# Up projections of a Mamba-2 and attention decoder: hi and lo of the input in one 512-column matmul, the two weights in banks of two pools

## The chip, the cores and the metric

The kernel runs on 1 core of one Trainium2 chip. The metric is the device time of one execution in microseconds; the median of 3 runs stands for the kernel.

## What is computed

A decoder of two layers on 256 tokens of width 1024, in float32. Each layer is a SwiGLU FFN (half step), a token mixer and another FFN; the mixer is a Mamba-2 scan in the first layer and sliding-window attention in the second. The change concerns the four FFNs alone:

```python
D_MODEL, SEQ, D_FF = 1024, 256, 2816

def swiglu_half_step(h, g, w1, w3, w2):
    u = rmsnorm(h, g)
    return h + 0.5 * ((silu(u @ w1) * (u @ w3)) @ w2)

h = swiglu_half_step(h, ...)      # layer 0, FFN 0
h = h + mamba2_mixer(...)
h = swiglu_half_step(h, ...)      # layer 0, FFN 1
k, v = shared_kv(h, ...)
h = swiglu_half_step(h, ...)      # layer 1, FFN 0
h = h + sliding_window_attention(...)
h = swiglu_half_step(h, ...)      # layer 1, FFN 1
```

## The kernel before, in words

Activations are kept transposed, features on the 128 partitions and the 256 tokens along the columns. To keep float32 accuracy every operand is split into two float32r parts, hi and lo, and a product is three matmuls: hi weight by hi input, hi weight by lo input, lo weight by hi input (`wmm3`, line 140). The input of the later up projections is split into `uTh` and `uTl` (lines 89 and 90) by `Norm.normalize` (line 291); the first two chunks use an input that is not yet normalized (`cur.vh`, `cur.vl`) and scale the result.

Weights come from HBM as 1 MB units (`Unit`, line 146) into one of 3 raw buffers, issued by SP; ScalarE casts the hi part (line 168) and VectorE subtracts to get the lo part (line 169), in pieces of 512 columns, into 8 hi and 8 lo buffers of 1024 columns.

An FFN (`run_ffn`, line 303) goes over 11 chunks of 256 hidden columns, c = 0 to 10, and two halves f of 128 columns each. For one half, `up` (line 355) makes w1 and w3 (w = 0 and 1) over eight k of 128 features. Both results share one bank of 512 columns, tile `pm`, w1 in the left half and w3 in the right. The bank comes from pool `ps_mm`, which has 2. `gate` (line 324) does silu of the left half on ScalarE (`sl`, line 330), the product with the right half on VectorE (`g`, line 332), and splits it into hi and lo, the two halves of tile `ghl` (ScalarE line 335, VectorE line 336). `flush` (line 378) then does the down projection of the half chunk before, 24 matmuls into four banks `acc`; in the last FFN it is 12 matmuls of 512 columns, with the gated product as the stationary operand and the weights streaming (`down_t`, line 372). At the end of an FFN the last two half chunks are projected down bank by bank.

A scheduler sets the order on each engine; some places are tied by hand. PSUM has eight banks: 2 of `ps_mm`, 4 of `ps_acc`, 2 of `ps_tr`. In the FFNs `ps_tr` serves small tiles only (the statistics of the norm, transposes). The core of it before the change:

```python
        def up(c, f):
            pm = ps_mm.tile([P, 512], F32, tag="mm", name=nm("pm"))
            ...
            for w in range(2):
                for k in range(KT):
                    up_one(c, f, pm, k, w, k == 0, k == KT - 1)
            return pm
```

Of the kernel before, what the change touches and what calls it, by code (L numbers as in the profile page):

```python
# [11 lines left out]
F32 = mybir.dt.float32  # L12
F32R = mybir.dt.float32r
AF = mybir.ActivationFunctionType
# [4 lines left out]
P = 128  # L19
D = 1024  # L20
KT = D // P
S = 256
# [18 lines left out]
def yoco_kernel(ctx: ExitStack, tc: tile.TileContext, a: dict, out: bass.AP):  # L41
    nc = tc.nc
    ctx.enter_context(nc.allow_low_precision("float32 operands split into float32r parts"))

    const = ctx.enter_context(tc.tile_pool(name="const", bufs=1))
# [3 lines left out]
    sb = ctx.enter_context(tc.tile_pool(name="sb", bufs=2))  # L49
    ps_mm = ctx.enter_context(tc.tile_pool(name="ps_mm", bufs=2, space=PSUM))  # L50
    ps_acc = ctx.enter_context(tc.tile_pool(name="ps_acc", bufs=4, space=PSUM))
    ps_tr = ctx.enter_context(tc.tile_pool(name="ps_tr", bufs=2, space=PSUM))
# [33 lines left out]
                            base=1 - P, channel_multiplier=1)  # L86

    hT = const.tile([P, KT, S], F32, name="hT")
    uTh = const.tile([P, KT, S], F32R, name="uTh")
    uTl = const.tile([P, KT, S], F32R, name="uTl")  # L90

    uid = [0]

    def nm(s):
        uid[0] += 1
        return f"{s}_{uid[0]}"
# [5 lines left out]
    def in_turn(op, *args, **kw):  # L102
        if strict[0]:
            with tc.issue_after(pe[-1]):
                r = op(*args, **kw)  # L105
        else:
            r = op(*args, **kw)  # L107
        pe.append(r.ins)

    def mm(o, l, r, first, last):  # L110
        in_turn(nc.tensor.matmul, o, l, r, start=first, stop=last)
# [18 lines left out]
    def tick():  # L130
        while soon and len(pe) >= soon[0][0]:
            soon.pop(0)[1]()
# [7 lines left out]
    def wmm3(o, wh, wl, uh, ul, first, last):  # L140
        mm(o, wh, uh, first, False)
        mm(o, wh, ul, False, False)
        mm(o, wl, uh, False, last)
        tick()
# [35 lines left out]
    def up_unit(w1, w3, c, half, cut=1, hold=False, between=None):  # L180
        cs = slice(c * 256, c * 256 + 256)
        n = 4 // cut
        parts = []
        for k in range(0, 4, n):
            r0 = half * 512 + k * P
            for i, w in enumerate((w1, w3)):
                parts.append((i * 256, 256, 512,
                              w[r0:r0 + n * P, cs].rearrange("(k p) c -> p k c", p=P), k))
            if between is not None and k == 0:
                parts.append(between)  # L190
        return Unit(parts, hold=hold)
# [44 lines left out]
    def two(ap):  # L236
        return ap.unsqueeze(1).to_broadcast([P, 2, S])

    def half(ap):
        return ap.rearrange("p (i s) -> p i s", i=2)  # L240
# [62 lines left out]
    def run_ffn(layer, j, cur, nxt, hook=None, ups=None, at=(60, 84), pre=None):  # L303
# [10 lines left out]
        def units(c):  # L314
            if c not in ups:
                ups[c] = [up_unit(w1, w3, c, 0), up_unit(w1, w3, c, 1)]
            return ups[c]
# [6 lines left out]
        def gate(c, pm):  # L324
            if c < 2:
                t = sb.tile([P, 512], F32, tag="cv", name=nm("tp"), bufs=2)
                nc.vector.tensor_mul(half(t), half(pm), two(cur.rb))
                pm = t
            sl = sb.tile([P, 256], F32, tag="g", name=nm("sl"), bufs=3)
            nc.scalar.activation(sl, pm[:, 0:256], AF.Silu)  # L330
            g = sb.tile([P, 256], F32, tag="g", name=nm("g"), bufs=3)
            nc.vector.tensor_mul(g, pm[:, 256:512], sl)  # L332
            ghl = sb.tile([P, 512], F32R, tag="ghl", name=nm("ghl"), bufs=4)
            gh, gl = ghl[:, 0:256], ghl[:, 256:512]
            nc.scalar.copy(gh, g)  # L335
            nc.vector.tensor_sub(gl, g, gh.bitcast(F32))
            return gh, gl

        def up_one(c, f, pm, k, w, first, stop):
            xh, xl = (cur.vh, cur.vl) if c < 2 else (uTh, uTl)  # L340
            wh, wl = units(c)[k // 4].get((k % 4) * 512 + w * 256 + f * P, P)
            wmm3(pm[:, w * 256:(w + 1) * 256], wh, wl, xh[:, k, :], xl[:, k, :], first, stop)

        def up_first():
            pms = [ps_acc.tile([P, 512], F32, tag="acc", name=nm("pm")),
                   (ps_acc if pre else ps_mm).tile([P, 512], F32, tag="acc" if pre else "mm", name=nm("pm"))]
            for k in range(KT):
                if pre and k in pre:
                    pre[k]()
                for f in range(2):  # L350
                    for w in range(2):
                        up_one(0, f, pms[f], k, w, k == 0 and w == 0, k == KT - 1 and w == 1)
            return pms

        def up(c, f):
            pm = ps_mm.tile([P, 512], F32, tag="mm", name=nm("pm"))
            if c == 1 and f == 0 and pre:
                for k in range(KT):
                    for w in range(2):
                        up_one(c, f, pm, k, w, k == 0 and w == 0, k == KT - 1 and w == 1)  # L360
# [5 lines that stand above are left out]
# [34 lines left out]
        def start_gates():  # L400
            for f in range(2):
                pend.append((0, f, gate(0, g0[f])))
            cur.normalize()

        slow = at[1] > 96
        for c in range(NCHUNK):
            for f in range(2):
                if c == 0 and f == 0:
                    later(*stats)
                    later(*scale)  # L410
                    with tc.issue_after(pe[-1]) if pe else nullcontext():
                        g0 = up_first()
                    if not slow:
                        start_gates()
                if c == 0:
                    continue
                pm = up(c, f)
                if slow and c == 1 and f == 0:
                    start_gates()
                g = gate(c, pm)  # L420
                if c < C:
                    if not (slow and c == 1 and f == 0):
                        flush(pend.pop(0))
                    if c == 1 and f == 1:
                        while pend:
                            flush(pend.pop(0))
                    pend.append((c, f, g))
                elif f == 0:
                    gc0 = g
                if c == 5 and len(gcols) == 1:  # L430
                    gain_cols(grow[1])
                if c == 5 and f == 0 and last:
                    residual()
                if c >= 3 and hook is not None:
                    next(hook, None)
# [10 lines left out]
        for t in range(NT):  # L446
            for n in range(2):
# [3 lines left out]
                o = sb.tile([P, 512], F32, tag="cv", name=nm("o"), bufs=2)  # L451
# [684 lines left out]
    def keep_x():  # L1136
# [17 lines left out]
        for b in (3, 0, 1, 2):  # L1154
# [4 lines left out]
    turn_x(0)  # L1159
    turn_x(1)  # L1160
    run_ffn(0, 0, norms[0], norms[1], ups=ups, at=(128, 142),
            pre={1: lambda: turn_x(2), 3: lambda: turn_x(3), 7: keep_x})
    xpool.close()
    with tc.tile_pool(name="mp", bufs=1) as mp:
        mamba(mp, norms[1], norms[2])
    with tc.tile_pool(name="ap", bufs=1) as ap:
        run_ffn(0, 1, norms[2], norms[3])
        kT, vtok, bias = {}, {}, {}
        run_ffn(1, 0, norms[3], norms[4], hook=shared_kv(ap, norms[3], kT, vtok, bias))
        attention(ap, norms[4], kT, vtok, bias, norms[5])  # L1170
# [40 lines left out]
```

## Time and profile before

| what | us |
| --- | --- |
| median of 3 runs | 1064.51 |
| the 3 runs | 1062.97, 1064.51, 1064.96 |
| profiled execution | 1061.67 |
| its span, first to last instruction | 1060.0 |

A name such as `pm<-uTh,wh` is the tile written and the tiles read, buffer numbers left out. PE is TensorE, PEld its weight loads, DVE VectorE, ACT ScalarE, POOL GpSimd. Matmuls overlap, so the length of one is not the time until the next starts: for the pace, divide a piece of the chain by its count, or subtract starts in the timeline. In a timeline row that merges several instructions the length is from the first start to the last end. `L107` is the line of a helper that issues nearly all matmuls, so matmuls are told apart by their tiles.

### The profile page before, as it was taken

How to read it: one execution, taken by the hardware profiler on the slowest of the kernel's cores; microseconds unless marked ns; L12 is line 12 of the kernel's file. 1: busy time of each engine (PE TensorE's matmuls, PEld its weight loads, DVE VectorE, ACT ScalarE, POOL GpSimd, SP SyncE). 2: the span in 40 equal slices, each digit the busy share in tenths (PEclk: the TensorE clock that was granted, in tenths of full speed). 3: DMA queues.
4: the chain of work that ended last, by engine and by line, in shares of the span. 5: the costliest groups of instructions: out<-in, count | busy, mean ns of one | idle time of the engine just before them, and what ended most of it. 6: DMA issues, size and time to landing. Idle time of an engine off the chain costs nothing.

```text
span 1060.0 us, 20512 instructions
## 1 busy us (share of the span) xinstructions
PE 1044.2 (99%) x8282; PEld 1006.2 (95%) x8282; DVE 701.4 (66%) x1420; ACT 582.7 (55%) x1204; POOL 53.0 (5%) x79
## 2 busy tenths in 40 slices
PE   9999999999999999999999999999999999999998
PEld 8999999989899999999999999999996699999997
DVE  6864545797899899645455974654577678454543
ACT  7553544677867656535445754454467565443541
POOL 1100000003210010000000000100002000000000
PEclk9999999999999999999999999999999999999999
DMA  8665646545456374646465556584641346463631
GB/s 290 207 211 177 207 161 219 169 146 197 147 169 222 120 194 168 199 163 221 161 213 164 195 162 198 165 297 162 213 159 41 120 136 216 149 216 124 227 127 40
DMA packets 138927, 187.34 MB, mean 177 GB/s; under 512 B 4940, under 2 KB 120816, under 8 KB 138832
## 3 DMA queue, kind: packets, MB, share of 16 engines
q1 hardware_dynamic: 136496, 179.32, 51.5%
q0 software_dynamic: 2288, 6.69, 2.2%
q8 instruction: 65, 1.06, 0.4%
q14 instruction: 30, 0.25, 0.1%
q10 hardware_dynamic: 48, 0.02, 0.0%
HBM read 184.90 MB, written 1.11 MB: 175 GB/s over the span
## 4 chain that ended last, share of the span: by engine, by line
PE 93%; DVE 4%; ACT 1%; DMA 1%; issue 1%; POOL 0%; SPq 0%; ACTq 0%; DVEq 0%; POOLq 0%
PE pm L107 47%; PE acc L107 23%; PE pp L107 8%; PE pa L107 5%; PE pq L105 2%; PE pa L105 1%; DVE wl L169 1%; PE pz L107 1%; PE py L107 1%; PE ps L105 1%; PE po L105 1%; DVE sp L961 1%; DMA xin<-in_x_dram 1%; PE pkv L107 1%; DVE zs L746 1%
## 5 line engine op out<-in xcount | busy, mean ns | idle before, releaser
L169 DVE TENSOR_TENSOR wl<-raw,wh 128x512 fp32r<-128x512 f32 x676 | 431.6, 685 | 140.9 <-ACT wh L168 140.1
L168 ACT CAST wh<-raw 128x512 fp32r<-128x512 f32 x676 | 379.1, 618 | 191.2 <-PE pm L107 89.4
L107 PE MATMUL pm<-uTh,wh 128*128 128x256 f32 x1152 | 323.2, 281 | 0.0
L107 PE MATMUL pm<-uTl,wh 128*128 128x256 f32 x1152 | 323.1, 280 | 0.0
L107 PE MATMUL pm<-uTh,wl 128*128 128x256 f32 x1152 | 323.1, 280 | 0.0
L107 PEld LDWEIGHTS pm<-uTh,wh 128*128 128x128 f32 x1152 | 217.2, 189 | 0.9 <-issue 0.2
L107 PEld LDWEIGHTS pm<-uTl,wh 128*128 128x128 f32 x1152 | 216.8, 188 | 0.6
L107 PEld LDWEIGHTS pm<-uTh,wl 128*128 128x128 f32 x1152 | 217.1, 188 | 0.0
L107 PE MATMUL acc<-ghl,wh 128*128 128x256 f32 x1056 | 190.9, 282 | 0.2 <-ACT ghl L335 0.2
L107 PEld LDWEIGHTS acc<-ghl,wh 128*128 128x128 f32 x1056 | 162.2, 188 | 0.4 <-ACT ghl L335 0.4
L107 PE MATMUL acc<-ghl,wl 128*128 128x256 f32 x528 | 148.6, 282 | 0.0
L332 DVE TENSOR_TENSOR g<-pm,sl 128x256 f32<-128x256 f32 x72 | 30.3, 421 | 134.7 <-ACT sl L330 134.7
L330 ACT ACTIVATE sl<-pm 128x256 f32<-128x256 f32 x72 | 27.4, 380 | 165.4 <-PE pm L107 165.4
L107 PEld LDWEIGHTS acc<-ghl,wl 128*128 128x128 f32 x528 | 99.4, 188 | 0.0
L107 PE MATMUL pp<-uTh,wh 128*128 128x256 f32 x288 | 81.8, 285 | 1.9 <-ACT uTh L300 1.4
L107 PE MATMUL pp<-uTl,wh 128*128 128x256 f32 x288 | 81.4, 284 | 0.4 <-DVE uTl L301 0.2
L107 PE MATMUL pp<-uTh,wl 128*128 128x256 f32 x288 | 80.8, 282 | 0.0
L107 PE MATMUL pm<-vh,wh 128*128 128x256 f32 x256 | 73.2, 286 | 0.0
L107 PE MATMUL pm<-vl,wh 128*128 128x256 f32 x256 | 72.4, 283 | 0.0
L107 PE MATMUL pm<-vh,wl 128*128 128x256 f32 x256 | 72.3, 283 | 0.0
L107 PE MATMUL acc<-wh,ghl 128*128 128x512 f32 x176 | 58.1, 394 | 0.0
L107 PEld LDWEIGHTS pp<-uTh,wh 128*128 128x128 f32 x288 | 54.4, 190 | 2.6 <-ACT uTh L300 1.5
(242 smaller groups left out, 1432.1 us busy)
## 6 DMA issues: line engine op xcount, KB each, us to landing
raw<-in_ffn_w_dram SPq DMA_DIRECT2D x168, 512.0 KB, 4.8
raw<-in_ffn_w_dram SPq DMA_DIRECT2D x44, 1024.0 KB, 5.1
raw<-in_ssm_w_in_dram SPq DMA_DIRECT2D x16, 1024.0 KB, 5.5
raw<-in_ssm_w_out_dram SPq DMA_DIRECT2D x8, 1024.0 KB, 5.2
raw<-in_ffn_w_dram SPq DMA_DIRECT2D x16, 256.0 KB, 6.0
raw<-in_ssm_w_in_dram SPq DMA_DIRECT2D x8, 512.0 KB, 5.4
pr<-pdram POOLq DMA_DIRECT2D x8, 512.0 KB, 4.6
raw<-in_w_q_dram SPq DMA_DIRECT2D x4, 1024.0 KB, 4.9
```

The lines of the kernel that those rows point to most:

```text
L105: r = op(*args, **kw)
L107: r = op(*args, **kw)
L168: return (nc.scalar.copy(wh, rs).ins, nc.vector.tensor_sub(wl, rs, wh.bitcast(F32)).ins)
L169: nc.vector.tensor_sub(wl, rs, wh.bitcast(F32)).ins)
L330: nc.scalar.activation(sl, pm[:, 0:256], AF.Silu)
L332: nc.vector.tensor_mul(g, pm[:, 256:512], sl)
L746: nc.vector.tensor_mul(zs[:, j, :], y1, zs[:, j, :])
L961: chain[1] = op(*args, **kw).ins
```

## The change

The hi and lo inputs become the two halves of one tile `uT`, side by side for each k. For chunks 2 to 10 the hi weight is multiplied with both at once, one matmul of 512 columns into a whole bank, so that the bank's left half gets hi by hi and its right half hi by lo; the lo weight by the hi input is added onto the left half by a second matmul of 256 columns. w1 and w3 then need a bank each, one of `ps_mm` and one of `ps_tr`. In the gate ScalarE copies the right half of each bank to SBUF and VectorE adds it to the left half (tile `tp`), before the silu and the product. Chunks 0 and 1, the down projections and the mixers compute as before.

```diff
--- before.py
+++ after.py
@@ -86,8 +86,8 @@
                             base=1 - P, channel_multiplier=1)
 
     hT = const.tile([P, KT, S], F32, name="hT")
-    uTh = const.tile([P, KT, S], F32R, name="uTh")
-    uTl = const.tile([P, KT, S], F32R, name="uTl")
+    uT = const.tile([P, KT, 2, S], F32R, name="uT")
+    uTh, uTl = uT[:, :, 0, :], uT[:, :, 1, :]
 
     uid = [0]
 
@@ -326,10 +326,19 @@
                 t = sb.tile([P, 512], F32, tag="cv", name=nm("tp"), bufs=2)
                 nc.vector.tensor_mul(half(t), half(pm), two(cur.rb))
                 pm = t
+            if c < 2:
+                p1, p3 = pm[:, 0:256], pm[:, 256:512]
+            else:
+                t = sb.tile([P, 512], F32, tag="cv", name=nm("tp"), bufs=2)
+                p1, p3 = t[:, 0:256], t[:, 256:512]
+                for o, pw in ((p1, pm[0]), (p3, pm[1])):
+                    lo = sb.tile([P, 256], F32, tag="g", name=nm("lo"), bufs=3)
+                    nc.scalar.copy(lo, pw[:, 256:512])
+                    nc.vector.tensor_add(o, pw[:, 0:256], lo)
             sl = sb.tile([P, 256], F32, tag="g", name=nm("sl"), bufs=3)
-            nc.scalar.activation(sl, pm[:, 0:256], AF.Silu)
+            nc.scalar.activation(sl, p1, AF.Silu)
             g = sb.tile([P, 256], F32, tag="g", name=nm("g"), bufs=3)
-            nc.vector.tensor_mul(g, pm[:, 256:512], sl)
+            nc.vector.tensor_mul(g, p3, sl)
             ghl = sb.tile([P, 512], F32R, tag="ghl", name=nm("ghl"), bufs=4)
             gh, gl = ghl[:, 0:256], ghl[:, 256:512]
             nc.scalar.copy(gh, g)
@@ -337,9 +346,8 @@
             return gh, gl
 
         def up_one(c, f, pm, k, w, first, stop):
-            xh, xl = (cur.vh, cur.vl) if c < 2 else (uTh, uTl)
             wh, wl = units(c)[k // 4].get((k % 4) * 512 + w * 256 + f * P, P)
-            wmm3(pm[:, w * 256:(w + 1) * 256], wh, wl, xh[:, k, :], xl[:, k, :], first, stop)
+            wmm3(pm[:, w * 256:(w + 1) * 256], wh, wl, cur.vh[:, k, :], cur.vl[:, k, :], first, stop)
 
         def up_first():
             pms = [ps_acc.tile([P, 512], F32, tag="acc", name=nm("pm")),
@@ -352,7 +360,20 @@
                         up_one(0, f, pms[f], k, w, k == 0 and w == 0, k == KT - 1 and w == 1)
             return pms
 
+        def up_wide(c, f):
+            pms = [ps_mm.tile([P, 512], F32, tag="mm", name=nm("pm")),
+                   ps_tr.tile([P, 512], F32, tag="tr", name=nm("pm"))]
+            for w in range(2):
+                for k in range(KT):
+                    wh, wl = units(c)[k // 4].get((k % 4) * 512 + w * 256 + f * P, P)
+                    mm(pms[w], wh, uT[:, k].rearrange("p i s -> p (i s)"), k == 0, False)
+                    mm(pms[w][:, 0:256], wl, uTh[:, k, :], False, k == KT - 1)
+                    tick()
+            return pms
+
         def up(c, f):
+            if c >= 2:
+                return up_wide(c, f)
             pm = ps_mm.tile([P, 512], F32, tag="mm", name=nm("pm"))
             if c == 1 and f == 0 and pre:
                 for k in range(KT):
```

The order of instructions moves with it, at three places.

TensorE, in an up projection of the sixth chunk of the first FFN, before (`wh` and `wl` are buffers of hi and lo weights, each row one matmul):

```order
L107 MATMUL pm_1232<-uTh,wh_1251 128x256
L107 MATMUL pm_1232<-uTl,wh_1251 128x256
L107 MATMUL pm_1232<-uTh,wl_1252 128x256
L107 MATMUL pm_1232<-uTh,wh_1253 128x256
L107 MATMUL pm_1232<-uTl,wh_1253 128x256
L107 MATMUL pm_1232<-uTh,wl_1254 128x256
```

and in the changed kernel, at the same chunk, where the bank of w1 (`pm_1183`) is followed by that of w3 (`pm_1184`):

```order
L107 MATMUL pm_1183<-uT,wh_1203 128x512
L107 MATMUL pm_1183<-uT,wl_1204 128x256
L107 MATMUL pm_1183<-uT,wh_1205 128x512
L107 MATMUL pm_1183<-uT,wl_1206 128x256
...
L107 MATMUL pm_1184<-uT,wh_1188 128x512
L107 MATMUL pm_1184<-uT,wl_1189 128x256
```

Three rows of 256 columns on one bank have become two, one of 512 columns and one of 256, and w3 starts in another bank.

ScalarE, at the end of the first FFN, before (`sl_2391` is the silu of the last gate, `ghl_2395` the hi part of its product, and the casts are of weights for what comes next; x2 stands for two instructions):

```order
L168 CAST wh_2556<-raw_2552 128x512 x2
L168 CAST wh_2568<-raw_2566 128x512 x2
L168 CAST wh_2570<-raw_2566 128x512
L330 ACTIVATE sl_2391<-pm_2342 128x256
L168 CAST wh_2570<-raw_2566 128x512
L168 CAST wh_2746<-raw_2743 128x512
L335 CAST ghl_2395<-g_2393 128x256
```

and in the changed kernel (`pm_2205` and `pm_2206` are the two banks of the last up projection, `sl_2246` and `ghl_2250` the silu and the product's hi part):

```order
L336 COPY lo_2240<-pm_2205 128x256
L168 CAST wh_2411<-raw_2407 128x512 x2
L168 CAST wh_2423<-raw_2421 128x512 x2
L168 CAST wh_2425<-raw_2421 128x512
L336 COPY lo_2243<-pm_2206 128x256
L339 ACTIVATE sl_2246<-tp_2239 128x256
L168 CAST wh_2425<-raw_2421 128x512
L168 CAST wh_2601<-raw_2598 128x512 x2
L344 CAST ghl_2250<-g_2248 128x256
```

The copy of the first bank stands ahead of five casts, the copy of the second behind them, where the silu was; between the silu and the hi part stand three casts where there were two.

TensorE, at the same end of the FFN, before (`ghl_2339` and `ghl_2395` are the products of the first and second half of chunk 10; `wh_2426` and `wh_2428` the weights of either, four banks `acc`):

```order
L107 MATMUL acc_516<-ghl_2339,wh_2426 128x256 x2
L107 MATMUL acc_516<-ghl_2339,wl_2427 128x256
L107 MATMUL acc_516<-ghl_2395,wh_2428 128x256 x2
L107 MATMUL acc_516<-ghl_2395,wl_2429 128x256
...
L107 MATMUL acc_517<-ghl_2339,wh_2426 128x256 x2
L107 MATMUL acc_517<-ghl_2339,wl_2427 128x256
```

and in the changed kernel, in the same place (`ghl_2202` and `ghl_2250` are the two products):

```order
L107 MATMUL acc_515<-ghl_2202,wh_2281 128x256 x2
L107 MATMUL acc_515<-ghl_2202,wl_2282 128x256
L107 MATMUL acc_515<-ghl_2250,wh_2283 128x256
L107 MATMUL acc_516<-ghl_2202,wh_2281 128x256 x2
L107 MATMUL acc_516<-ghl_2202,wl_2282 128x256
L107 MATMUL acc_516<-ghl_2250,wh_2283 128x256
L107 MATMUL acc_517<-ghl_2202,wh_2281 128x256
L107 MATMUL acc_515<-ghl_2250,wh_2283 128x256
L107 MATMUL acc_515<-ghl_2250,wl_2284 128x256
```

Before, 128 output features were finished with both halves of the chunk before the next 128 began. Now matmuls of the first half's product, and those of the second half's hi part, are taken ahead from the next banks; the first that reads the lo part of `ghl_2250` is the last but one of these rows.

## Rows read from the trace of the kernel before

**Rows 1.** The page, parts 1 and 2: the span, busy time of each engine with its share of the span, and the granted clock of TensorE in 40 slices, in tenths.

```profile
span 1060.0 us, 20512 instructions
PE 1044.2 (99%) x8282; PEld 1006.2 (95%) x8282; DVE 701.4 (66%) x1420; ACT 582.7 (55%) x1204; POOL 53.0 (5%) x79
...
PEclk9999999999999999999999999999999999999999
```

**Rows 2.** The page, part 4: the chain that ended last, shares of the span by engine and by line.

```profile
PE 93%; DVE 4%; ACT 1%; DMA 1%; issue 1%; POOL 0%; SPq 0%; ACTq 0%; DVEq 0%; POOLq 0%
PE pm L107 47%; PE acc L107 23%; PE pp L107 8%; PE pa L107 5%; PE pq L105 2%; PE pa L105 1%; DVE wl L169 1%; PE pz L107 1%; PE py L107 1%; PE ps L105 1%; PE po L105 1%; DVE sp L961 1%; DMA xin<-in_x_dram 1%; PE pkv L107 1%; DVE zs L746 1%
```

**Rows 3.** What TensorE waited for: us in total, times, longest.

```profile
PE pa L107 <- DVE wl L169: 1.8, 1, 1.8
...
PE acc L107 <- ACT ghl L335: 0.2, 1, 0.2
```

**Rows 4.** The page, part 5: groups of matmuls and weight loads, with count, busy us and mean ns of one.

```profile
L107 PE MATMUL pm<-uTh,wh 128*128 128x256 f32 x1152 | 323.2, 281 | 0.0
L107 PE MATMUL pm<-uTl,wh 128*128 128x256 f32 x1152 | 323.1, 280 | 0.0
L107 PE MATMUL pm<-uTh,wl 128*128 128x256 f32 x1152 | 323.1, 280 | 0.0
L107 PEld LDWEIGHTS pm<-uTh,wh 128*128 128x128 f32 x1152 | 217.2, 189 | 0.9 <-issue 0.2
...
L107 PE MATMUL acc<-wh,ghl 128*128 128x512 f32 x176 | 58.1, 394 | 0.0
```

**Rows 5.** The chain in order of time, in the second FFN: start us, length us, what, count.

```profile
447.79 5.63 PE pm L107 x48
453.42 2.85 PE acc L107 x24
456.28 5.69 PE pm L107 x48
461.97 2.85 PE acc L107 x24
```

**Rows 6.** The same chain in the last FFN.

```profile
896.64 5.70 PE pm L107 x48
902.34 2.78 PE acc L107 x12
905.12 5.70 PE pm L107 x48
```

**Rows 7.** The same chain, the opening chunks of the second FFN (input vh and vl) and the query projection.

```profile
398.31 7.19 PE pm L107 x60
...
405.83 2.98 PE pm L107 x24
...
781.95 9.53 PE pq L105 x42
```

**Rows 8.** The timeline of TensorE in a down projection of the last FFN: start us, us from first start to last end, what, count.

```profile
902.65 0.62 PE L107 MATMUL acc<-wh,ghl 128*128 128x512 f32 x2
903.11 0.40 PE L107 MATMUL acc<-wl,ghl 128*128 128x512 f32 x1
903.34 0.64 PE L107 MATMUL acc<-wh,ghl 128*128 128x512 f32 x2
903.81 0.39 PE L107 MATMUL acc<-wl,ghl 128*128 128x512 f32 x1
```

**Rows 9.** Instructions on the gate's tile sl: count, duration ns least, median and most, first and last start us, forms.

```profile
L330 ACT ACTIVATE sl<-pm x72: 372/383/387, 51.4 to 1047.2; 128x256 f32<-128x256 f32 x72
L332 DVE TENSOR_TENSOR g<-pm,sl x72: 413/423/427, 52.2 to 1047.7; 128x256 f32<-128x256 f32 x72
```

**Rows 10.** Busy us and instructions of each engine in a stretch of steady chunks of the second FFN: stretch, its length, PE, PEld, DVE, ACT, POOL, then TensorE's clock, DMA share, GB/s.

```profile
447.80:565.00 117.20, 117.20 (x993) 117.20 (x993) 60.43 (x108) 53.57 (x109) 0.00 (x0) 1.00 0.57 188
```

**Rows 11.** The timeline of TensorE at the end of the first FFN: its first down matmuls, and the first that read the last gate's product.

```profile
191.52 0.40 PE L107 MATMUL acc<-ghl,wh 128*128 128x256 f32 x2
...
194.73 0.40 PE L107 MATMUL acc<-ghl,wh 128*128 128x256 f32 x2
```

**Rows 12.** The timeline of ScalarE at the same place, with the idle time before and its releaser.

```profile
189.46 2.71 ACT L168 CAST wh<-raw 128x512 fp32r<-128x512 f32 x5 [2.10 <-PE pm L107]
192.07 0.37 ACT L330 ACTIVATE sl<-pm 128x256 f32<-128x256 f32 x1
192.35 1.13 ACT L168 CAST wh<-raw 128x512 fp32r<-128x512 f32 x2
193.38 0.41 ACT L335 CAST ghl<-g 128x256 fp32r<-128x256 f32 x1
```

**Rows 13.** The timeline of VectorE at the same place.

```profile
190.12 2.50 DVE L169 TENSOR_TENSOR wl<-raw,wh 128x512 fp32r<-128x512 f32 x4 [2.29 <-ACT wh L168]
192.53 0.42 DVE L332 TENSOR_TENSOR g<-pm,sl 128x256 f32<-128x256 f32 x1
192.87 1.28 DVE L169 TENSOR_TENSOR wl<-raw,wh 128x512 fp32r<-128x512 f32 x2
194.07 0.42 DVE L336 TENSOR_TENSOR ghl<-g,ghl 128x256 fp32r<-128x256 f32 x1
```

## The prediction

> **What bounds the kernel now.** I read the busy times first, then the chain that ended last, then what TensorE waits for, then the chain in order of time. TensorE is busy for 99% of the span and its granted clock stands at the upper of its two levels, 2.4 GHz, in every slice [rows 1]. The chain that ended last is 93% TensorE, and the up projections (tile pm on line 107) alone are 47% of it [rows 2]. TensorE's own waits are short: the longest is 1.8 us and the only one before a down projection 0.2 us [rows 3]. So an edit is worth what it takes from TensorE's stream of matmuls, plus any wait that it opens.
>
> A busy share says nothing of the pace of the stream, because matmuls overlap: one is shown as 281 ns long, a wide one of 512 columns as 394 [rows 4]. The pace is read from the chain, as length over count. In the second FFN (the first and third read alike) the 48 narrow (256-column) matmuls of an up projection take 5.63 us for one half of a chunk and 5.69 for the other, 117.3 and 118.5 ns each, and 24 of a down projection take 2.85 us, 118.8 each [rows 5]. In the last FFN an up takes 5.70 us, 118.8 each, and the 12 wide matmuls of its down projection 2.78 us, 231.7 ns each [rows 6]. Each of these loads its own weights. The query projection, wide too, takes 9.53 us for 42, 226.9 each [rows 7].
>
> **The change, part by part.**
>
> *Fewer matmuls.* The edit concerns chunks 2 to 10 of four FFNs: 9 x 2 x 4 = 72 up projections, each of 16 steps (two weights, eight k). That is the 1152 of [rows 4]. A step was three narrow matmuls and becomes one wide and one narrow; the columns streamed stay at 768, and one weight load and one matmul go. Before: (3 x (117.3 + 118.5) / 2 + 118.8) / 4 = 118.1 ns for a narrow one over the four FFNs, 354.4 for a step. After: 231.7 + 118.1 = 349.8. Saved: 4.6 ns x 1152 = **5.3 us**. No row has wide and narrow matmuls in turn, so both ends: the best pace of either shape is 226.9 + 117.3 = 344.2, saving 11.8 us; the worst is a wide matmul at 235 (the pair that starts at 903.34 takes 0.47 us up to the next start [rows 8]) and a narrow one at 124.2 (24 in 2.98 us, from an opening chunk on vh and vl [rows 7]), 359.2, a loss of 5.5 us. I take the middle because its rows are nearest: same engine line, same float32r operands, in an FFN between up projections.
>
> The Trainium skill, "TensorE: Matmul & The Clock Gate", section "Back-to-back issue gap", puts a warm matmul at N/2.4 + 2.5 ns, so that one matmul less at equal columns saves 2.5 ns; my estimate by it is 1152 x 2.5 = 2.9 us in place of 5.3. This trace does not agree in size: the fixed part is 2 x 118.1 - 231.7 = 4.5 ns, and both shapes are slower than the formula.
>
> *The halves are added afterwards.* Each of the 72 gates gains two ScalarE copies out of PSUM and two VectorE adds. The nearest rows have the same shapes and the same kind of operands: the silu out of pm, 383 ns, and the product with one operand in PSUM, 423 ns [rows 9]. In all 144 x 0.383 = 55 us on ScalarE and 144 x 0.423 = 61 us on VectorE. In the 117.2 us of steady chunks in [rows 10] VectorE is busy 60.43 and ScalarE 53.57, so in a chunk of 17.02 us (two ups and two downs) 8.8 and 7.8. The edit adds 4 x 0.423 = 1.7 and 4 x 0.383 = 1.5: 10.5 and 9.3, still under two thirds. Cost on TensorE's stream: nothing, as long as no consumer is late. That holds in mid-FFN: the product of a gate is consumed after the previous down projection and a whole up projection, 2.85 + 5.6 = 8.5 us after its own up ends, and a gate now ends about 3 us after it (next paragraph). Behind the waiting copies in ScalarE's queue stand the casts of the next chunk's weights; four of them stand between the first copy and the second, as they stood ahead of the silu before, and they wait for a weight buffer that the same up projection frees, so they start no later. They are consumed 2.85 us and more after the up ends, and end about 0.65 us after it.
>
> *The end of an FFN.* Here the cover is thin: after the last up there are 24 matmuls of the previous half chunk and 3 of chunk 10's first half, and then the last gate's product is read. Take the first FFN, with T = 191.52, the start of the down matmuls [rows 11]. TensorE reads the last product at 194.73, T + 3.21. ScalarE's five casts end at T + 0.65, its part gh of the product at T + 2.27 [rows 12], VectorE's part gl at T + 2.97 [rows 13]. After the change, with the rows' own starts: copy T + 0.55 to 0.94, add to 1.39, one weight subtraction, product to about 2.3; ScalarE meanwhile does silu, then three casts to 2.8, gh to about 3.15; VectorE does two weight subtractions and gl to about 3.8. The new order puts matmuls that don't need gl ahead of those that do (shown with the change): gl is read 33 matmuls after T, 33 x 0.1188 = T + 3.92. So it fits by 0.1 us, and I book 0.1 for each of the three FFNs that end so, **0.3 us**; from below it is 0, from above the 1 us by which the gate got longer, 3 us in all. The last FFN has no casts behind its last unit and a wider cover: nothing.
>
> *Banks.* An up projection takes one bank from each of two pools of two. The bank of one up is taken again two ups later, over 8 us after its last read; nothing is booked. *Layout.* hi and lo in one tile change strides and no instruction's size: nothing. *Queues.* SP's transfers stand in the same order, POOL has the same 82 rows; a chunk is 0.15 us shorter in 17, which asks nothing of the transfers.
>
> Sum: -5.3 + 0.3 = **-5.0 us**. The profiled execution took 1061.67 us, 1.67 around a span of 1060.0, and would come to 1056.7. It lies 2.84 below the median of the runs, 1064.51, so I forecast **1059.5** for the median.
>
> **Rivals.**
>
> *A wide matmul costs two narrow ones*: no change. It needs 236.2 ns where two averages read 226.9 and 231.7; for it speaks that the same narrow shape reads from 117.3 to 124.2 in different surroundings [rows 5, 7], a spread larger than the 4.6 ns at stake. Time: 1064.5 + 0.3 = 1064.8. I count here all outcomes within 0.2% (2.1 us, about what a measurement of this kernel can tell from no change). Chance 0.20.
>
> *The alternation falls on the slow side*: wide 235, narrow 124.2, as priced above, +5.5 + 0.3: 1070.3, slower. It decides once a step takes more than 354.4 + 1.6 = 356.0 ns. Against it: 235 is the worst pair of a down projection and 124.2 comes from an opening chunk; each would have to become the rule. Chance 0.08.
>
> *The alternation falls on the fast side*: 344.2 a step, 1064.5 - 11.8 = 1052.7. For it: the query projection holds 226.9 over 42 matmuls. Chance 0.13.
>
> *Weight loads set the pace.* Then a wide matmul with one load would pass at the pace of a narrow one: a step of 236.2 ns, 118.2 x 1152 = 136 us less, 928. The load engine is busy 95% of the span [rows 1]; but wide matmuls with one load each take 231.7 ns, so the columns set the pace and not the loads. Chance 0.01. It is what the Trainium skill, "Perfetto Trace Analysis", section "Identifying the Most-Contended Engine", would lead to, which judges TensorE by the busy share of LDWEIGHTS rather than of matmuls; by that a third of the up projections' loads is the thing to remove, and the wide rows here disagree.
>
> **How the numbers follow.** My forecast has the remaining 0.58. Faster by over 0.2% is forecast, fast side and weight loads, 0.72; the same 0.20; slower 0.08. The range goes from the fast side, 1052, to just over no change, 1065; it leaves out the slow side, the weight loads and the edges of the cases at its ends, under 0.2 together.
>
> **What would show it.** Right: 1152 wide matmuls on pm; an up projection of 32 matmuls in about 5.6 us of the chain (16 x 349.8 ns) where 48 took 5.63 to 5.70; down projections still 2.85; TensorE's waits before acc under 1 us; VectorE about 762 us busy, ScalarE about 638. Wrong: ups of 5.5 us (fast side) or 5.75 (slow side); new waits of TensorE for the gate's tiles ghl or for wl; or a wait before pm for its two banks, which I book at nothing.

## The result

The changed kernel took 1054.05 us, the median of four runs, beside 1063.74 for the kernel before on the same chip: ratio 0.9919, interval 0.9898 to 0.9939. Timed once more, in a later batch, it took 1053.00 beside 1061.62: 0.9923, 0.9904 to 0.9941. The medians lie 9.7 and 8.6 us apart, and both ratios stand for about 8.6 us, where 5.0 was forecast. The ratios here are estimates from the fast runs and not quotients of the medians, and they leave out one slow execution, of 1441 us at a granted clock of 0.655, in the run with three narrow matmuls. The execution profiled first took 1054.95 us, with a span of 1053.2.

The page of the changed kernel, its span, busy times and granted clock (to set against [rows 1]), and then its groups that are new or changed ([rows 4, 9]):

```profile
span 1053.2 us, 18596 instructions
...
PE 1037.4 (98%) x7130; PEld 950.7 (90%) x7130; DVE 760.0 (72%) x1564; ACT 628.1 (60%) x1348; POOL 54.5 (5%) x79
...
PEclk9999999999999999999999999999999999999999
...
L107 PE MATMUL pm<-uT,wh 128*128 128x512 f32 x1152 | 402.9, 392 | 0.0
L107 PE MATMUL pm<-uT,wl 128*128 128x256 f32 x1152 | 321.7, 280 | 0.0
...
L336 ACT COPY lo<-pm 128x256 f32<-128x256 f32 x144 | 53.3, 370 | 211.0 <-PE pm L107 211.0
L337 DVE TENSOR_TENSOR tp<-pm,lo 128x256 f32<-128x256 f32 x144 | 60.8, 422 | 154.4 <-ACT lo L336 154.4
```

TensorE is as full as it was, with 1152 matmuls fewer; VectorE and ScalarE have new groups of 61 and 53 us, and with 72% and 60% are still far from full. The weight loads' share fell from 95% to 90%. "PE ... <- ..." is what TensorE waits for, in the next view (us in total, times, longest; to set against [rows 3]):

```profile
PE px L1146 <- DMA xin<-in_x_dram: 1.9, 2, 1.6
PE pa L107 <- DVE wl L169: 1.8, 1, 1.8
...
```

The other waits of the list are shorter, 1.5 us and less. No wait for the gate's tiles, for wl in an FFN or for a bank of pm has come in. What did change is the chain in order of time, in the second FFN (start us, length us, what, count; [rows 5] before). The chain of this execution can be followed back unbroken only to the state-space stage; for what lies ahead of it, the chain of the repeat is used below.

```profile
480.02 5.55 PE pm L107 x32
485.57 2.85 PE acc L107 x24
```

and in the last FFN ([rows 6] before):

```profile
892.24 5.56 PE pm L107 x32
897.80 2.77 PE acc L107 x12
```

An up projection takes 5.55 us where it took 5.63 and 5.69; in the last FFN 5.56 where it took 5.70. A step is 5.55 / 16 = 346.9 ns against 5.66 / 16 = 353.8, and 347.5 against 356.3. Over the 54 ups of three FFNs and 18 of the last that is 54 x 0.11 + 18 x 0.14 = 8.5 us. The down projections kept their pace.

The ends of the FFNs gave a little back. The 72 down matmuls of the second FFN's end, before and then after:

```profile
578.29 8.54 PE acc L107 x72
```

```profile
575.12 8.80 PE acc L107 x72
```

The first and third read 8.55 to 8.74 (in the repeat) and 8.54 to 8.75: 0.7 us in all. 8.5 - 0.7 = 7.8, against the starts of the stages, where the four FFNs shrink by 8.0. To see that, take the chain of the repeat (the second timing of the changed kernel)

```profile
198.19 5.75 PE pz L107 x48
394.87 7.19 PE pm L107 x60
581.62 7.20 PE pm L107 x60
775.04 9.53 PE pq L105 x42
857.65 7.18 PE pm L107 x60
```

beside that of the kernel before, whose second FFN and query projection stand in [rows 7]:

```profile
200.34 5.74 PE pz L107 x48
...
586.82 7.19 PE pm L107 x60
...
864.27 7.18 PE pm L107 x60
```

The first FFN ends 2.15 us earlier, the second is 1.76 shorter (186.75 against 188.51), the third 1.71 (193.42 against 195.13), and from the last opening to the end of the span (1051.0 and 1060.0) it is 2.38 less. The same account over the whole trace, adding for each matmul the time from its start to the next start: the later up projections take 400.3 us in the repeat against 408.6 before, the down projections 253.4 against 252.8.

### The profile page after: what moved, and what is told of

Read it like the earlier page. It is cut to its first block, busy times and chain, and to the rows that moved or that the text cites. A ratio compares the mean times of both kernels' runs of the same rounds, so it can differ in the third digit from the quotient of the medians.

```text
span 1053.2 us, 18596 instructions
## 1 busy us (share of the span) xinstructions
PE 1037.4 (98%) x7130; PEld 950.7 (90%) x7130; DVE 760.0 (72%) x1564; ACT 628.1 (60%) x1348; POOL 54.5 (5%) x79
## 4 chain that ended last, share of the span: by engine, by line
PE 72%; issue 21%; DVE 4%; POOL 1%; DMA 1%; ACT 1%; SPq 0%; POOLq 0%; DVEq 0%; ACTq 0%
PE pm L107 37%; PE acc L107 18%; PE pa L107 5%; PE pp L107 5%; PE pq L105 2%; PE pa L105 1%; PE ps L105 1%; DVE wl L169 1%; PE py L107 1%; DVE sp L982 1%; PE po L105 1%; DMA xin<-in_x_dram 1%; PE pkv L107 1%; ACT em L607 1%; DVE zs L767 1%
## 5 line engine op out<-in xcount | busy, mean ns | idle before, releaser
L107 PE MATMUL pm<-uT,wh 128*128 128x512 f32 x1152 | 402.9, 392 | 0.0
L107 PE MATMUL pm<-uT,wl 128*128 128x256 f32 x1152 | 321.7, 280 | 0.0
L107 PEld LDWEIGHTS pm<-uT,wh 128*128 128x128 f32 x1152 | 216.1, 188 | 45.7 <-issue 0.2
L107 PEld LDWEIGHTS pm<-uT,wl 128*128 128x128 f32 x1152 | 216.5, 188 | 1.1 <-DVE wl L169 0.2
L336 ACT COPY lo<-pm 128x256 f32<-128x256 f32 x144 | 53.3, 370 | 211.0 <-PE pm L107 211.0
L337 DVE TENSOR_TENSOR tp<-pm,lo 128x256 f32<-128x256 f32 x144 | 60.8, 422 | 154.4 <-ACT lo L336 154.4
L107 PE MATMUL pp<-uT,wh 128*128 128x256 f32 x576 | 107.1, 287 | 2.2 <-ACT uT L300 1.4
L107 PEld LDWEIGHTS pp<-uT,wh 128*128 128x128 f32 x576 | 90.4, 192 | 3.1 <-ACT uT L300 1.5
L107 PE MATMUL pp<-uT,wl 128*128 128x256 f32 x288 | 81.5, 284 | 0.0
L107 PEld LDWEIGHTS pp<-uT,wl 128*128 128x128 f32 x288 | 55.1, 191 | 0.0
```

The costliest lines, as they stand in the source:

```text
L336: nc.scalar.copy(lo, pw[:, 256:512])
L337: nc.vector.tensor_add(o, pw[:, 0:256], lo)
```

## The experiments

All times are medians beside runs of the kernel before on the same chip; ratios are to those. The quoted expectations use letters. At first there were three theories. **A**: the stream pays for its columns and a fixed part for each matmul, so the gain is the 1152 matmuls that are gone. **B**: the layout or the banks of two pools bring it. **C**: the weight loads set the pace. **D**, formed after the first runs, joins two of them: a matmul takes what its columns take, but never less than the load of its weights.

**Three narrow matmuls again**, with the new layout, banks and gate kept.

```diff
-  mm(pms[w], wh, uT[:, k].rearrange("p i s -> p (i s)"), k == 0, False)
+  mm(pms[w][:, 0:256], wh, uTh[:, k, :], k == 0, False)
+  mm(pms[w][:, 256:512], wh, uTl[:, k, :], False, False)
```

> The changed kernel with its wide matmul split again into two narrow ones (hi weight by hi input into the left half, hi weight by lo input into the right half); tile uT, the two banks and the gate with its copies and adds stay. Theory A, a fixed part per matmul: the step goes from the 347.4 ns measured after back to three narrow, 354.4 (118.1 each), +7.0 ns x 1152 = +8.1 us on the changed kernel, about 1062, ratio to the kernel before 0.999 to 1.001. Theory B, the gain comes from the layout or the two banks and the narrow pace follows them: stays at the changed kernel's time, ratio 0.992. Theory C, weight loads set the pace: back to three loads, as A.

Measured: 1061.38 us, ratio 1.0002 (0.9988 to 1.0016). Its chain in the second FFN is that of [rows 5] again:

```profile
449.28 5.63 PE pm L107 x48
...
457.77 5.69 PE pm L107 x48
```

The whole gain hangs on the wide matmul; layout, banks and gate bring nothing, and cost nothing that shows in the time (its FFN ends, the 72 down matmuls, read 8.83 to 8.86 us in place of 8.54).

**The banks alone**, in the kernel before (narrow matmuls, w1 and w3 each in a bank of its own pool, no halves to add).

```diff
+  pms = [ps_mm.tile([P, 256], F32, tag="mm", name=nm("pm")),
+         ps_tr.tile([P, 256], F32, tag="tr", name=nm("pm"))]
...
```

> The kernel before with one part of the change alone: w1 and w3 in chunks 2 to 10 in a bank each, of two pools, 256 columns wide; three narrow matmuls, no halves to add, uTh and uTl as before. Theory A and C: no change, ratio 0.998 to 1.002. Theory B in its form with banks: a share of the 0.8% appears here, ratio 0.992 to 0.997, with narrow matmuls at 117 ns or less in every up projection.

Measured: 1061.31, ratio 0.9996 (0.9984 to 1.0008), ups of 5.63 and 5.69. B is out from both sides.

**No adding of the halves**: the gate reads the first half of each bank.

```diff
-  for o, pw in ((p1, pm[0]), (p3, pm[1])):
...
-      nc.scalar.copy(lo, pw[:, 256:512])
-      nc.vector.tensor_add(o, pw[:, 0:256], lo)
+  p1, p3 = pm[0][:, 0:256], pm[1][:, 0:256]
```

> The changed kernel without the copies and adds of the gate; it leaves out the product of hi weight and lo input in chunks 2 to 10. It shows what the adding of the halves costs. Theory A and B alike: the down projections at the end of the first three FFNs go from 8.80 us back to 8.55, 0.25 x 3, and VectorE's and ScalarE's other work comes a little earlier: 0.5 to 1.5 us less than the changed kernel, ratio to before 0.9905 to 0.9915. Rival: the adding costs more than that somewhere else on the path, 2 us or more less: ratio 0.990 or below.

Measured: 1053.81, ratio 0.992 (0.9903 to 0.9937), the changed kernel's own. The 0.5 to 1.5 us less that was expected is neither shown nor ruled out by this interval. 144 copies and 144 adds, 114 us of engine time, cost no more than that. They do show at the FFN's end, which is back at its old length:

```profile
575.10 8.54 PE acc L107 x72
```

**The narrow matmul in two of 128 columns.** The columns stay; each step gets one weight load and one matmul more.

```diff
-  mm(pms[w][:, 0:256], wl, uTh[:, k, :], False, k == KT - 1)
+  mm(pms[w][:, 0:128], wl, uTh[:, k, 0:128], False, False)
+  mm(pms[w][:, 128:256], wl, uTh[:, k, 128:256], False, k == KT - 1)
```

> The changed kernel with the lo weight's narrow matmul split into two of 128 columns: same columns, one matmul and one weight load more per step. Theory A: one fixed part more, 5 to 6 ns x 1152 = 6 to 7 us more than the changed kernel, ratio to before 0.998 to 0.999. Theory C, a weight load needs about the 115 ns of a narrow matmul whatever is streamed: the step goes from 347 to 230 + 2 x 115 = 460 ns, +130 us, ratio 1.11. Theory B: says nothing against A here.

Measured: 1183.54, ratio 1.1147 (1.1119 to 1.1175), 130 us over the changed kernel. The chain:

```profile
480.36 7.29 PE pm L107 x48
```

A step is 7.29 / 16 = 455.6 ns, 109 more than with one narrow matmul. If the wide one still takes 230, the two short ones take 113 each in the mean; the starts themselves are uneven (287 ns from the wide one to the first short one, 58 to the second, 111 to the next wide one). The weight loads' timeline points to the reason (start us, from first start to last end):

```profile
480.89 0.19 PEld L107 LDWEIGHTS pm<-uT,wl 128*128 128x128 f32 x1
481.00 0.19 PEld L107 LDWEIGHTS pm<-uT,wh 128*128 128x128 f32 x1
481.11 0.42 PEld L107 LDWEIGHTS pm<-uT,wl 128*128 128x128 f32 x2
481.45 0.19 PEld L107 LDWEIGHTS pm<-uT,wh 128*128 128x128 f32 x1
```

Loads start 0.11, 0.23 and 0.11 us apart and never closer. A fixed part of a few ns per matmul cannot give 109; the same columns in twice the matmuls cost nearly twice the time. A is wrong for narrow matmuls, and D was formed here. A rival would be a floor of some 110 ns under every matmul, whatever its weights. Other matmuls of the kernel speak against it. The repeat's timeline has four that stream one column through 128 columns of weights (tile pc):

```profile
401.78 0.53 PEld L107 LDWEIGHTS pc<-mean,sq 128*128 128x128 f32 x4
```

With one load 0.19 long, these four start (0.53 - 0.19) / 3 = 0.11 us apart, as beside 128 columns streamed. Matmuls that stream 128 columns through only 64 columns of weights (tile py, in the state-space stage) start 50 to 59 ns apart there, four in a row. So it is not a floor of matmuls as such; it goes with the weights.

D has two ends to test: fewer columns should help a wide matmul fully and a narrow one hardly.

**The narrow matmul with 192 columns** (it leaves out the product for the last 64 tokens).

```diff
-  mm(pms[w][:, 0:256], wl, uTh[:, k, :], False, k == KT - 1)
+  mm(pms[w][:, 0:192], wl, uTh[:, k, 0:192], False, k == KT - 1)
```

> The changed kernel with the lo weight's matmul cut from 256 to 192 columns; it leaves out the lo weight's product for the last 64 tokens in chunks 2 to 10. Loads and matmuls stay in number. Theory A, columns plus a fixed part: 64 columns x 0.44 ns (230 - 117.5 over 256) = 28 ns less per step, x 1152 = 32 us less than the changed kernel, ratio to before 0.962. Theory D, formed after the run with 128 columns twice (three loads and two short matmuls took 456 ns, not 354): a matmul can't follow the one before sooner than a weight load of some 113 ns, and a narrow one stands at that floor already: at most 4 ns less per step, 0 to 5 us, ratio 0.987 to 0.992.

**The wide matmul with 448 columns**, for seven of eight k.

```diff
-  mm(pms[w], wh, uT[:, k].rearrange("p i s -> p (i s)"), k == 0, False)
+  m = 512 if k == 0 else 448
+  mm(pms[w][:, 0:m], wh, uT[:, k].rearrange("p i s -> p (i s)")[:, 0:m], k == 0, False)
```

> The changed kernel with the hi weight's matmul cut from 512 to 448 columns for seven of eight k; it leaves out the product of hi weight and lo input for the last 64 tokens there. The same 64 columns as in the run with 192, taken from the other matmul. Theory A and D alike: 28 ns x 1008 = 28 us less than the changed kernel, ratio to before 0.965. Theory C, loads set the pace everywhere: no change, 0.992.

Measured: 1051.80, ratio 0.991 (0.9888 to 0.9932), and 1027.47, ratio 0.9679 (0.9656 to 0.9703). An up of the first and then of the second:

```profile
520.86 5.42 PE pm L107 x32
```

```profile
526.15 5.20 PE pm L107 x32
```

With 64 columns less the wide matmul gives back 0.35 us an up, 25 ns for each of the 14 shortened ones; 72 x 0.35 = 25.2 us is the gain over the changed kernel's 1053.00 (25.5), and C by itself, which expected none, is out. The narrow one gives back 0.13 us, 8 ns each. If the wide one keeps its 230, the floor of the narrow one is near 347 - 8 - 230 = 109 ns, which is what the split matmul cost. D holds for the step as a whole; the starts share the time out otherwise (250 ns from wide to narrow, 91 from narrow to wide). Most of the 72 x 0.13 = 9.4 us that the 192 columns should still bring is not in the time. Added from start to next start over the whole trace, the later up projections do take 392.3 us against 400.3 in the repeat, but the down projections take 259.8 against 253.4 and everything else 298.8 against 297.3. In the down projections there is a wait at three FFN ends that the changed kernel doesn't have, since the order there came out otherwise:

```profile
PE acc L107 <- ACT ghl L344: 4.2, 3, 1.4
```

**Wide twice**: the lo weights stream hi and lo inputs as well (this adds the product of the lo parts).

```diff
-  mm(pms[w][:, 0:256], wl, uTh[:, k, :], False, k == KT - 1)
+  mm(pms[w], wl, uT[:, k].rearrange("p i s -> p (i s)"), False, k == KT - 1)
```

> The changed kernel with the lo weight's matmul widened to 512 columns too (it adds the product of both lo parts). Two loads per step as before, 1024 columns in place of 768. Theory A and D: 2 x 230 = 460 ns per step, +112 ns x 1152 = +129 us on the changed kernel, about 1183. Theory C: no change. It also gives the pace of wide matmuls with no narrow one between: 227 to 232.

Measured: 1191.35, ratio 1.122 (1.1187 to 1.1252), about as A and D expected.

```profile
523.92 7.50 PE pm L107 x32
```

Wide matmuls in a row take 7.50 / 32 = 234.4 ns each, above the 227 to 232 that were expected. Had one cost that in the changed kernel, beside a narrow one at 117 or 118, a step would take 352 and not 347. So a wide matmul among narrow ones is cheaper here. Three orders of the same 32 matmuls test that. The first was put on record together with the run above and sets **E**, that the pace of a shape depends on its neighbours, against A and D. The other two came after it. **F** says that a wide neighbour on one side, the next or the previous, makes a wide matmul dear, so that in twos half of them pay. **G** says that only long runs pay. **H** says that the turn itself is what counts, and **J**, that it is the input which the two matmuls of a step share.

**Eight wide, then eight narrow.**

```diff
-  for k in range(KT):
+  for i in range(2):
+      for k in range(KT):
...
+          if i == 0:
+              mm(pms[w], wh, uT[:, k].rearrange("p i s -> p (i s)"), k == 0, False)
+          else:
+              mm(pms[w][:, 0:256], wl, uTh[:, k, :], False, k == KT - 1)
```

> The changed kernel with the eight wide matmuls of a weight first and then its eight narrow ones, in place of turn and turn about; nothing else. Theory A and D: the same step, ratio to before 0.991 to 0.993. Rival E, the pace of a shape depends on its neighbours (the narrow shape read 117.3 to 124.2 in the kernel before): wide ones among themselves at 226.9 as in the query projection, 3 us less, or narrow ones among themselves at 118.2 as before, 1 us more.

**Two wide, then two narrow.**

```diff
+  for k in range(0, KT, 2):
...
+      for i in range(2):
+          mm(pms[w], hl[i][0], uT[:, k + i].rearrange("p i s -> p (i s)"), k + i == 0, False)
+      for i in range(2):
+          mm(pms[w][:, 0:256], hl[i][1], uTh[:, k + i, :], False, k + i == KT - 1)
```

> The changed kernel with the turns taken two by two: wide, wide, narrow, narrow. One at a time the step is 347 ns (wide 229.9), eight at a time 352 (wide 234.1). Theory F, a wide matmul loses its 4 ns where the next or the previous matmul is wide too: half of the wide ones lose, step 349.5, +2.4 us on the changed kernel, and starts in the trace that read 230 and 234 in turn. Rival G, only long runs of wide ones lose: as the changed kernel.

**In turn, but shifted**: the wide matmul of k + 1 ahead of the narrow one of k, so that neighbours share no input.

```diff
...
+  for k in range(KT + 1):
+      if k < KT:
+          mm(pms[w], hl[k][0], uT[:, k].rearrange("p i s -> p (i s)"), k == 0, False)
+      if k > 0:
+          mm(pms[w][:, 0:256], hl[k - 1][1], uTh[:, k - 1, :], False, k == KT)
```

> The changed kernel with the narrow matmuls one k later: wide k+1, then narrow k, still in turn (but for the first two wide and the last two narrow of each weight). In the changed kernel a wide matmul and the narrow one behind it stream the same hi columns; here they stream different ones. The runs with turns of two and of eight took 352 ns per step, the changed kernel 347. Theory H, the turn itself gives the 5 ns: 7 of 8 steps keep it, step about 347.5, ratio 0.992 to 0.993. Rival J, the same input in both gives it: step about 352, ratio 0.997 to 0.998.

Measured, in this order: 1057.53, ratio 0.9962 (0.9949 to 0.9975); 1059.76, ratio 0.9979 (0.9968 to 0.9991); 1053.87, ratio 0.9932 (0.9914 to 0.995). An up of each, in the second FFN:

```profile
521.06 5.62 PE pm L107 x32
```

```profile
523.88 5.63 PE pm L107 x32
```

```profile
528.08 5.57 PE pm L107 x32
```

That is 351.3, 351.9 and 348.1 ns a step. The grouped order missed what A and D expected (0.991 to 0.993), and E's two prices as well (3 us less or 1 us more). Pairs lose as much as runs of eight, so F and G both fall: the full price is back as soon as wide ones stand in twos. The shifted order, which breaks the turn once at each end of a bank's row of 16, keeps nearly all of it. So it is the turn itself (H) and not the input that neighbours share (J). The starts in the traces say more closely what the turn is. With a narrow matmul on both sides a wide one takes 229.5 ns to the next start (1076 in the repeat). In the pairs the first wide one takes 232.8 and the second 234.6, and the two that meet in the shifted order take 232.4 and 233.0 where its others take 229.6. A wide neighbour on either side is enough, here in the up projections. It isn't a law for all wide matmuls: 42 in a row of the query projection take 226.9 each [rows 7], and what differs there was not tested. The turn is worth 351.6 - 346.9 = 4.7 ns a step, 1152 x 4.7 = 5.4 us, and the same 32 matmuls in groups save only some 2 to 4 us over the kernel before. Why the turn is cheaper the traces don't show, and it stays open.

**The changed kernel once more**, beside the pairs.

> The changed kernel itself, unchanged, on the chip of the next two runs: a ratio to the kernel before with more runs behind it. All theories: inside the first interval, 0.990 to 0.994; the chain's step at 347 ns.

Measured: 1053.00, as told above, with ups of 5.55 us.

**Chunk 1 wide as well**, for seven of its eight up projections; its gate scales the summed halves.

```diff
...
-  mm(pms[w], wh, uT[:, k].rearrange("p i s -> p (i s)"), k == 0, False)
-  mm(pms[w][:, 0:256], wl, uTh[:, k, :], False, k == KT - 1)
+  x = cur.v if c == 1 else uT
+  mm(pms[w], wh, x[:, k].rearrange("p i s -> p (i s)"), k == 0, False)
+  mm(pms[w][:, 0:256], wl, x[:, k, 0, :], False, k == KT - 1)
...
```

> The changed kernel with chunk 1 wide too (seven of its eight up projections; hi and lo of the not yet normalized input in one tile, and the halves added before the scaling). 7 x 16 = 112 steps of three narrow matmuls at 120 become 347: 13 ns x 112 = 1.5 us less than the changed kernel, if VectorE, which then normalizes as well, takes two more adds per gate beside it. Rival: the down projections of chunks 0 and 1 wait for the gates and it comes out 1 us or more slower than the changed kernel.

Measured: 1051.44, ratio 0.9907 (0.9889 to 0.9925), beside 0.9923 for the changed kernel in the same batch. It beats the kernel before; that it beats the changed kernel too is likely and not resolved, since the intervals overlap. Its chain in the second FFN's opening

```profile
406.95 7.08 PE pm L107 x44
...
416.91 5.55 PE pm L107 x32
```

stands beside 7.19 for 60 and 5.75 for 48 in the changed kernel: 0.11 and 0.20 less. That is about 1 us over the seven up projections (0.8 by the starts of all matmuls on pm, 493.6 us against 494.3), where 1.5 was expected; its median is 1.6 below the changed kernel's.

## Why the prediction came out as it did

*Direction and mechanism were right.* TensorE's stream bounds the kernel before and after, and the gain is what the up projections lost. Undoing the wide matmul alone brings the old time back (1.0002, 0.9988 to 1.0016).

*The costs put at nothing don't show.* Banks and layout: 0.9996 and 1.0002. The gate: VectorE 760 us and ScalarE 628, forecast as 762 and 638, no wait in mid-FFN, and the same time without copies and adds, within the intervals.

*The step that failed in size is "Fewer matmuls".* It put a step at 349.8 ns from 354.4, 4.6 saved, 5.3 us in all. Measured is 346.9 (347.5 in the last FFN), 6.9 to 8.8 saved, 8.5 us. The price that was off is above all the wide matmul's: 231.7, from a row of wide matmuls among themselves. In the up projection wide ones in a row cost 234, and in turn with narrow ones 230 (the mean from a wide one's start to the next start; for the narrow one 117.5, where 118.1 was booked). The forecast took a price from the right shape and operands, and from the wrong neighbours. Chosen rightly by its own rule (nearest surroundings) there was no row to take, as the prediction said; what it could not know was that the turn has a price of its own, which by these runs is more than half of the gain. That the forecast came as near as it did is in part luck: without the turn its own rows would have promised too much (orders without it save 2 to 4 us), and with it they promised too little. By the step the result lies halfway between the forecast and the fast-side rival, which had 344.2; by the time it is nearer to that rival's 1052.7 than to 1059.5. Part of that last distance is the base: the forecast stood on a median of 1064.51 of three runs, where the kernel before took 1061.4 to 1063.7 in all later comparisons. Single executions of 1063 to 1065 us stand in these only with a mean granted clock of 0.994 or 0.995, so the three of the base were probably of that kind; their clocks are not on record.

*What the prediction said of the pace was half right.* It said that columns set it and not the loads. The 448-column run shows that for the wide matmul (25 ns for 64 columns), and the split and the 192-column runs show that the narrow one stands only 8 ns above its load's floor. So the "fixed part of 4.5 ns" that it worked out from 2 x 118.1 - 231.7 is no fixed part of a matmul. The Trainium skill, "TensorE: Matmul & The Clock Gate", section "LDWEIGHTS (loading the stationary operand)", gives a load in ns as its columns / 1.2, an estimate of 107 ns for 128 columns; the 109 ns that a further 128-column matmul cost here agrees with it. Its section "Back-to-back issue gap", whose formula is for a matmul by itself and by which the estimate was 2.9 us, comes close to the orders without the turn (1.9 and 4.2 us below the kernel before), and not to the turn's 8.6.

*The FFN's end was placed rightly and priced low.* Forecast 0.1 each, measured 0.19 to 0.26. Here is the first FFN's end with T = 189.11, ScalarE, VectorE and TensorE after the change ([rows 11 to 13] before):

```profile
189.72 0.36 ACT L336 COPY lo<-pm 128x256 f32<-128x256 f32 x1
...
190.30 1.66 ACT L168 CAST wh<-raw 128x512 fp32r<-128x512 f32 x3
191.85 0.41 ACT L344 CAST ghl<-g 128x256 fp32r<-128x256 f32 x1
```

```profile
190.18 0.41 DVE L337 TENSOR_TENSOR tp<-pm,lo 128x256 f32<-128x256 f32 x1
...
192.65 0.41 DVE L345 TENSOR_TENSOR ghl<-g,ghl 128x256 fp32r<-128x256 f32 x1
```

```profile
189.11 0.40 PE L107 MATMUL acc<-ghl,wh 128*128 128x256 f32 x2
...
192.31 0.62 PE L107 MATMUL acc<-ghl,wh 128*128 128x256 f32 x3
192.78 0.28 PE L107 MATMUL acc<-ghl,wl 128*128 128x256 f32 x1
192.90 0.61 PE L107 MATMUL acc<-ghl,wh 128*128 128x256 f32 x3
193.34 0.28 PE L107 MATMUL acc<-ghl,wl 128*128 128x256 f32 x1
```

The hi part ends at T + 3.15, as forecast, and the lo part at T + 3.95 where 3.8 was forecast and T + 3.92 allowed. TensorE takes 0.47 and 0.44 us for three matmuls there (192.31 to 192.78, 192.90 to 193.34), where three elsewhere take 0.36: 0.2 us lost at two places, just where the parts come in.

## What to carry to other kernels

Take the price of an instruction from a row with the same neighbours, not only with the same shape; where no such row exists, the order of the same instructions can be worth as much as dropping some of them, as it was here. Ask of each matmul whether its columns or its weight load set its pace before counting what fewer columns or fewer matmuls bring. Work put on engines that were about two thirds busy cost nothing here until the end of a stage, where the other work that covers it runs out.

## What the runs showed of the hardware

*Turn and group.* 512- and 256-column float32r matmuls strictly in turn took 346.9 ns a pair, in twos 351.9, in eights 351.3, at a granted clock of 1.00 in these stretches. A wide one took 229.5 ns with narrow ones on both sides and 232.4 to 234.6 with a wide one on either side.

*A weight load's floor.* One more matmul of 128 columns with weights of its own lengthened a step by 109 ns; one of 256 took 117. Loads of 128 columns of weights started 0.11 us apart whether one column was streamed behind each or 128.

*The granted clock of one stage explains the difference between two profiles of one kernel.* The same changed kernel, profiled first and in the repeat, in the state-space stage (stretch, length, TensorE's busy time and count, granted clock, DMA share, GB/s), at two places:

```profile
215.00:220.00 5.00, 4.76 (x25) 0.66 0.01 3
311.00:316.00 5.00, 4.70 (x26) 0.66 0.11 16
```

```profile
215.00:220.00 5.00, 4.64 (x35) 1.00 0.02 3
311.00:316.00 5.00, 5.00 (x44) 1.00 0.40 103
```

Ahead of the first place TensorE had waited 1.40 us for uT on ScalarE, in both. Behind that the clock was granted at 0.66 in the mean in the one, which puts part of the stretch at the lower level of 1.2 GHz, and stayed at 2.4 GHz in the other. The timelines of TensorE at the first place, first profile and repeat:

```profile
216.48 0.42 PE L107 MATMUL pp<-uT,wl 128*128 128x256 f32 x1
216.70 0.41 PE L107 MATMUL pp<-uT,wh 128*128 128x256 f32 x1
```

```profile
216.27 0.28 PE L107 MATMUL pp<-uT,wl 128*128 128x256 f32 x1
216.39 0.28 PE L107 MATMUL pp<-uT,wh 128*128 128x256 f32 x1
```

Matmuls of the same shape start 0.22 us apart in the one and 0.12 in the other. Matched one by one, the first profile falls 1.1 us behind the repeat at this place and 1.3 at the second. From the first pz (198.0, 197.9) to the second FFN (397.16, 394.87) the stage took 199.2 and 197.0 us, and 198.2 in the kernel before. The 2.2 us between the two profiles of one kernel lie there, and nothing of them comes from the change; the FFNs, where the clock is 1.00, are the place to compare. In the batch of the repeat the same shows in the times: five executions of the kernel before at a mean granted clock of 0.998 took 1060.2 to 1060.6 us and six at 0.995 took 1062.6 to 1064.4, while the changed kernel took 1052.7 and 1052.8 at 0.998 and 1055.6 at 0.995. At equal clock the gain is about 7.5 us, near the 8.0 of the chain.
